# Cosine attention on one core: three score chunks exponentiated on VectorE, six K products on VectorE, four buffers of exponentials

## The chip, the core and the metric

The kernel runs on one core of a Trainium2 chip. The metric is the device time of one execution in microseconds, as the median of three runs. The engines are TensorE (PE; its weight loads are PEld), VectorE (DVE), ScalarE (ACT), GpSimd (POOL) and SyncE (SP), whose queue issues nearly all the transfers. Each engine works off its own queue strictly in order, and semaphores order the engines among each other.

## The reference

Q, K and V have shape (8, 12, 512, 64) in float32, and tau is 0.1.

```python
Q_norm = Q / (np.linalg.norm(Q, axis=-1, keepdims=True) + 1e-10)
K_norm = K / (np.linalg.norm(K, axis=-1, keepdims=True) + 1e-10)
scores = np.einsum('bhqd,bhkd->bhqk', Q_norm, K_norm) / tau
weights = np.exp(scores - np.max(scores, axis=-1, keepdims=True))
weights = weights / (np.sum(weights, axis=-1, keepdims=True) + 1e-10)
return np.einsum('bhqk,bhkd->bhqd', weights, V).astype(np.float32)
```

A score is a cosine divided by 0.1, so it lies within 10 of zero, and the kernel leaves out the maximum: a factor common to a row drops out when the row is divided by its sum.

## The kernel before

The 96 heads are worked in 48 pairs (0 to 47), two heads side by side on the 128 partitions. For one pair:

- LD and LV load Q, K and V (SP's queue). SQ squares Q and K (GpSimd, 1024 columns), SSQ sums the squares with eight matmuls against the identity into PSUM bank "x", and RED (VectorE) adds the rest, into a slot of the norm scratch bank nps.
- NEW is a chain of Newton steps on VectorE that turns sums into reciprocal norms, for a group of two pairs at once; it keeps its data in nps too. Pairs 0 to 2 go through LN and EX on ScalarE instead.
- SCL multiplies Q (w = 0, VectorE) and K (w = 1, GpSimd for most pairs) by their reciprocal norms. TR transposes both on TensorE into PSUM (banks "x" and "o1"), EVA copies them out to qt (VectorE, L504).
- SCO.s.c is score chunk c of 4: two matmuls of 512 columns, one for each head, on different halves of the array's rows, into two of the four banks of scps. EXP.s.c (ScalarE, L542) exponentiates the chunk, 1024 columns, into et. A SCO can start when the EXP two chunks before it is over.
- PV multiplies et by V, 32 matmuls of 65 columns (the 65th column is of ones and gives the row sums), into banks "o0" and "o1". VC (GpSimd) converts V to bf16 into vb beforehand. RCP and NRM (VectorE) divide and write ob; ST stores it.

A pair has four EXP, so ScalarE's order is a plain row of chunks. Buffers go round in rings: 18 of Q and K and of vb, 5 of qn and qt, 3 of et (R_ET).

The order of every queue is written out by hand in the table ORDER, one list of names for each engine. `schedule` (line 45) reads it; `run` (line 59) then makes the waits: an operation names what it needs, and gets a semaphore wait for each need on another engine (on TensorE and ScalarE, needs on the same engine are dropped; on VectorE they are kept). An operation with `take` waits for the last reader of the PSUM bank.

`split` (line 593) is in the kernel before and unused there, since SPLIT (line 675) is empty. It computes an exponential without ScalarE: a score product is added to a constant level, so that the float32 word holds, in its upper and lower halves, the integer and fractional part of the exponent, and four VectorE instructions evaluate a cubic on the lower half and write the result as the bits of a bf16 number.

Of the kernel before, what the change touches and what calls it, by code (L numbers as in the profile page):

```python
# [28 lines left out]
class Program:  # L29
# [95 lines left out]
def bass_cosine_similarity_attention_kernel(  # L125
# [16 lines left out]
    R_QK, R_V, R_SQ, R_QN, R_QT, R_ET, R_O = 18, 6, 6, 5, 5, 3, 8  # L142
# [8 lines left out]
    vb = sb("vb", [128, R_QK, NT, 2, DIM + 1], bf16)  # L151
# [11 lines left out]
    level = sb("level", [128, 128 + SEQ], bf16)  # L163
    wd = [sb(f"wd{i}", [128, SEQ], f32) for i in range(2)]
# [51 lines left out]
    def scored(s):  # L216

        if s < 0:
            return []
        last = [("SCO", s, NT - 1) if s else ("SCO", 0, 1, NT - 1)]  # L220
        return last + [("SCD", s, h) for h in range(2) if s in SPLIT]

# [204 lines left out]
    def pair(s):  # L427
# [24 lines left out]
        if 0 < s < LOGS:  # L452
# [9 lines left out]
            for w, dst in ((0, rq), (1, r)):  # L462
                exps(s, (w,), dst, xl[s][:, w], ("LN", s), gain, free)
            scaled(s, 0, "dve", rq, [("EX", s, 0), ("EX", s, 1)])
            for j in range(2) if s == 1 else ():
                scaled(1, 1, eng, r, [("EX", 1, w) for w in range(2)], (j,), slice(2 * j, 2 * j + 2))
            if s > 1:
                scaled(s, 1, eng, r, [("EX", s, w) for w in range(2)])
        elif s:
# [5 lines left out]
            else:  # L475
                free = [("EX", LOGS - 1, w) for w in range(2)]
# [39 lines left out]
        for c in range(NT) if s else ():  # L516
# [23 lines left out]
            else:  # L540
# [5 lines left out]
        P.add(("VC", s), "pool", [("LV", s), key("PV", s - R_QK, 1, NT - 1), "vone"],  # L546
              lambda e: e.tensor_scalar(  # L547
                  out=vb[:, iq, :, :, 0:DIM].rearrange("p c h d -> p h c d"),
# [5 lines left out]
        for c in range(NT) if s in CHUNKED else ():  # L554
            def pv(e, c=c):
                for h in range(2):
                    for t in range(NT):
                        last = e.matmul(  # L558
                            out=o_ps[:, h, 65 * t : 65 * t + 65],
                            lhsT=et[iet][:, c, h, 128 * t : 128 * t + 128], rhs=vb[:, iq, c, h, :],  # L560
# [3 lines left out]
            P.add(("PV", s, c), "pe", [("EXP", s, c), ("VC", s), ("PV", s, c - 1) if c else None], pv,  # L564
                  take=[] if c else ["o0", "o1"], until=("NRM", s))
        for h in range(2) if s not in CHUNKED else ():
            for t in range(NT):
                def pv(e, h=h, t=t):
                    for c in range(NT):
                        last = e.matmul(  # L570
                            out=o_ps[:, h, 65 * t : 65 * t + 65],
                            lhsT=et[iet][:, c, h, 128 * t : 128 * t + 128], rhs=vb[:, iq, c, h, :],
# [5 lines left out]
                      [("EXP", s, NT - 1) if s else ("EXP", 0, 1, 1), ("VC", s), before,  # L578
                       *([("EXD", s, h, 3)] if s in SPLIT else []),
# [13 lines left out]
    def split(s, c, ready, iqt, iet):  # L593

        for h in range(2):
            hs = slice(64 * h, 64 * h + 64)

            def scd(e, hs=hs):
                e.matmul(out=x_ps[:, :], lhsT=level[hs, 0:128], rhs=level[hs, 128 : 128 + SEQ], start=True, stop=False)
                return e.matmul(out=x_ps[:, :], lhsT=qt[iqt][hs, 1, c, :], rhs=qt[iqt][hs, 0, :, :], start=False, stop=True)  # L600

            P.add(("SCD", s, h), "pe", ready + ["level"], scd, take=["x"], until=("EXD", s, h, 3))
            w, done = wd[len(exd) % 2], exd[-2:-1]
            steps = [
                lambda e, w=w: e.tensor_scalar(
                    out=w[:, :], in0=y_u, scalar1=1.0, scalar2=-65536.0, op0=ALU.mult, op1=ALU.add),
                lambda e, w=w: e.tensor_tensor(out=w[:, :], in0=y_u, in1=w[:, :], op=ALU.mult),
                lambda e, w=w: e.scalar_tensor_tensor(
                    out=w[:, :], in0=y_u, scalar=65536.0 * CUBIC[1], in1=w[:, :], op0=ALU.add, op1=ALU.mult),
                lambda e, w=w, h=h: e.scalar_tensor_tensor(  # L610
                    out=et[iet][:, c, h, :].bitcast(u16), in0=w[:, :], scalar=128 * CUBIC[0] / 65536.0**3, in1=x_ps[:, :],
                    op0=ALU.mult, op1=ALU.add)]
            for k, step in enumerate(steps):
                P.add(("EXD", s, h, k), "dve",
                      [("EXD", s, h, k - 1) if k else ("SCD", s, h)] + (done if k == 0 else [])
                      + ([key("PV", s - R_ET, 1, NT - 1)] if k == 3 else []), step)
            exd.append(("EXD", s, h, 3))

    def final(s, iq, iet, io):
# [3 lines left out]
        for i, (h, lo, hi) in enumerate(ENDS):  # L623
            for c in range(NT):
                def pv(e, i=i, h=h, c=c, lo=lo, hi=hi):
                    for t in range(lo, hi):
                        last = e.matmul(
                            out=bank[i][:, 65 * t : 65 * t + 65],
                            lhsT=et[iet][:, c, h, 128 * t : 128 * t + 128], rhs=vb[:, iq, c, h, :],
# [5 lines left out]
                       scores_read(place[s, NT - 1] - 1) if i == 2 else None, ("VC", s),  # L635
# [23 lines left out]
    if FILL[1]:  # L659
# [14 lines left out]
ON = {'SQ.0.0.1': 'pool', 'SCL.2.1': 'dve', 'SCL.3.1': 'dve', 'LD.1.1': 'sp', 'SCL.1.1': 'dve'}  # L674
SPLIT = {}
# [8 lines left out]
        LD.0.0.0 LD.0.0.1 LD.1.0 LD.1.1 LD.2.0 LD.2.1 LD.3.0 LD.3.1 LD.4.1 LV.0 LD.4.0 LD.5.0 LD.5.1 LV.1 LD.6.1  # L684
        LD.6.0 LD.7.0 LD.7.1 LD.9.0 LV.2 LD.9.1 LD.8.0 LV.3 LD.10.0 LD.8.1 LV.6 LD.10.1 LV.4 LD.11.0 LV.5 LD.12.0
        LD.11.1 LV.8 LD.12.1 LD.14.0 LD.13.0 LD.13.1 LD.18.0 LD.14.1 LV.10 LV.7 LD.21.0 LD.16.0 LD.16.1 LD.15.0 LV.9
# [171 lines left out]
```

## Time and profile before

| | |
|---|---|
| median of 3 runs | 191.3 us (191.04 to 191.97) |
| span of the profiled execution | 189.4 us; its own time is not listed beside the span |
| granted TensorE clock | 0.996 |
| busy: PE, DVE, ACT, POOL | 174.1, 148.1, 181.7, 160.7 us |
| EXP (L542) | 184 of 1024 columns, 169.1 us busy |
| first EXP of pair 0, last of all | begins at 7.64 us, ends at 186.26 us |

Busy time is the union of an engine's instruction spans; an instruction's span reaches into that of the next, so a group's mean is longer than the distance from one start to the next. A busy PE is not a PE at its peak, because ends of matmuls are modelled. In a row of groups stand line, engine, operation, tiles and shapes, count, then busy time and mean ns of one, then the idle time before and what ended it. In a row of the timeline stand start, length and instruction.

### The profile page before, as it was taken

How to read it: one execution, taken by the hardware profiler on the slowest of the kernel's cores; microseconds unless marked ns; L12 is line 12 of the kernel's file. 1: busy time of each engine (PE TensorE's matmuls, PEld its weight loads, DVE VectorE, ACT ScalarE, POOL GpSimd, SP SyncE). 2: the span in 40 equal slices, each digit the busy share in tenths (PEclk: the TensorE clock that was granted, in tenths of full speed). 3: DMA queues.
4: the chain of work that ended last, by engine and by line, in shares of the span. 5: the costliest groups of instructions: out<-in, count | busy, mean ns of one | idle time of the engine just before them, and what ended most of it. 6: DMA issues, size and time to landing. Idle time of an engine off the chain costs nothing.

```text
span 189.4 us, 7341 instructions
## 1 busy us (share of the span) xinstructions
PE 174.1 (92%) x3078; PEld 110.7 (58%) x3078; DVE 148.1 (78%) x453; ACT 181.7 (96%) x210; POOL 160.7 (85%) x147
## 2 busy tenths in 40 slices
PE   7989998999999998999999999989989999987893
PEld 5446664665665665666555666556656666654552
DVE  1999987879877886898876968969888787787624
ACT  5699999999999999999999999999999999999993
POOL 1799999999999999999999999999997599562500
PEclk9999999999999999999999999999999999999998
DMA  6999999999469999999999959899959500754435
GB/s 169 338 352 349 350 350 349 350 376 383 151 197 356 291 345 315 269 376 323 359 361 378 271 167 336 257 332 345 328 160 313 168 12 9 211 177 140 141 107 173
DMA packets 52448, 50.80 MB, mean 268 GB/s; under 512 B 3136, under 2 KB 52416, under 8 KB 52416
## 3 DMA queue, kind: packets, MB, share of 16 engines
q1 hardware_dynamic: 51984, 50.02, 82.3%
q8 instruction: 24, 0.39, 0.9%
q10 hardware_dynamic: 432, 0.33, 0.6%
q14 instruction: 8, 0.07, 0.1%
HBM read 37.75 MB, written 12.58 MB: 266 GB/s over the span
## 4 chain that ended last, share of the span: by engine, by line
ACT 82%; DVE 7%; PE 7%; DMA 1%; issue 1%
ACT et L542 80%; PE scps L526 2%; DMA qk<-in_Q_dram 1%; DVE qn L296 1%; PE bps L570 1%; DVE ob L586 1%; DVE qt L504 1%; ACT et L371 1%; PE bps L339 1%; PE bps L558 1%; DVE nps L276 1%; PE bps L268 1%; DVE ob L643 1%; PE bps L498 0%; DVE xs L324 0%
## 5 line engine op out<-in xcount | busy, mean ns | idle before, releaser
L542 ACT ACTIVATE et<-scps 128x1024 bf16<-128x1024 f32 x184 | 169.1, 1128 | 0.5 <-PE scps L526 0.4
L250 POOL TENSOR_TENSOR sq<-qk 128x1024 bf16<-128x1024 f32 (+2 forms) x48 | 87.9, 1848 | 5.1 <-DMA qk<-in_Q_dram 4.9
L526 PE MATMUL scps<-qt 64*128 64x512 bf16 x376 | 74.4, 385 | 8.4 <-ACT et L542 6.1
L570 PEld LDWEIGHTS bps<-vb,et 128*128 128x128 bf16 x1472 | 51.4, 98 | 24.1 <-issue 18.0
L570 PE MATMUL bps<-vb,et 128*128 128x65 bf16 x1472 | 65.1, 194 | 0.2
L296 POOL TENSOR_TENSOR qn<-qk,rk 128x512 bf16<-128x512 f32 x44 | 45.8, 1051 | 11.8 <-DVE rk L405 11.7
L504 DVE COPY qt<-bps 128x1024 bf16<-128x1024 bf16 x46 | 31.8, 691 | 10.1 <-PE bps L498 9.4
L296 DVE TENSOR_TENSOR qn<-qk,nps 128x512 bf16<-128x512 f32 (+1 forms) x51 | 33.9, 671 | 0.8 <-ACT nps L286 0.2
L586 DVE TENSOR_TENSOR ob<-bps,rd 128x512 f32<-128x512 f32 x47 | 32.5, 691 | 1.2
L526 PEld LDWEIGHTS scps<-qt 64*128 64x128 bf16 x376 | 18.2, 93 | 25.3 <-ACT et L542 13.4
L547 POOL TENSOR_SCALAR vb<-vf 128x512 bf16<-128x512 f32 x48 | 29.9, 634 | 0.0
L268 PE MATMUL bps<-sq,ident 128*128 128x128 bf16 x376 | 29.1, 220 | 0.0
L268 PEld LDWEIGHTS bps<-sq,ident 128*128 128x128 bf16 x376 | 21.2, 98 | 9.4 <-issue 6.3
L584 DVE RECIPROCAL rd<-bps 128x8 f32<-128x8 f32 x47 | 9.7, 207 | 17.7 <-PE bps L570 14.3
L498 PE MATMUL bps<-ident,qn 64*128 64x64 bf16 x736 | 18.8, 191 | 2.4 <-DVE ob L586 0.4
L498 PEld LDWEIGHTS bps<-ident,qn 64*128 64x128 bf16 x736 | 14.2, 95 | 9.8 <-DVE nps L276 4.0
L276 DVE TENSOR_REDUCE nps<-bps 128x16 f32<-128x128 f32 x45 | 13.4, 297 | 1.8 <-PE bps L268 1.8
L397 DVE TENSOR_TENSOR nps<-nps,ys 128x32 f32<-128x32 f32 (+1 forms) x48 | 9.2, 193 | 0.9
L401 DVE SCALAR_TENSOR_TENSOR nps<-nps,ys 128x32 f32<-128x32 f32 (+1 forms) x48 | 9.1, 191 | 0.8
L237 PE MATMUL scps<-warm_in 128*128 128x256 bf16 x22 | 4.8, 402 | 1.1 <-DVE warm_in L232 1.1
L409 DVE TENSOR_SCALAR ys<-nps 128x32 int32<-128x32 int32 (+1 forms) x24 | 4.4, 183 | 0.5
L405 DVE SCALAR_TENSOR_TENSOR nps<-nps,ys 128x16 f32<-128x16 f32 (+1 forms) x25 | 4.3, 175 | 0.3
(44 smaller groups left out, 47.4 us busy)
## 6 DMA issues: line engine op xcount, KB each, us to landing
vf<-in_V_dram SPq DMA_DIRECT2D x48, 256.0 KB, 5.4
qk<-in_Q_dram SPq DMA_DIRECT2D x47, 256.0 KB, 5.9
qk<-in_K_dram SPq DMA_DIRECT2D x47, 256.0 KB, 5.7
out_dram<-ob SPq DMA_DIRECT2D x47, 256.0 KB, 4.4
qk<-in_Q_dram SPq DMA_DIRECT2D x2, 128.0 KB, 2.7
qk<-in_K_dram ACTq DMA_DIRECT2D x2, 128.0 KB, 2.9
out_dram<-ob SPq DMA_DIRECT2D x1, 128.0 KB, 2.2
out_dram<-ob SPq DMA_DIRECT2D x1, 64.0 KB, 1.9
```

Of the source, the lines that this page charges most:

```text
L250: emit = lambda e: e.tensor_tensor(out=b, in0=a, in1=a, op=ALU.mult)
L268: last = e.matmul(out=ps[:, 0:128], lhsT=ident[:, :], rhs=sq[s % R_SQ][:, :, 8 * k : 8 * k + 8], start=(k == 0), stop=(k == 7))
L276: lambda e: e.tensor_reduce(out=dst(None), in_=ps[:, 0:128].rearrange("p (w g e) -> p w g e", w=2, e=8), axis=AX.X, op=ALU.add))
L296: lambda e: e.tensor_tensor(out=o, in0=x, in1=r, op=ALU.mult))
L498: last = e.transpose(t_ps[:, k, b, :], qn[s % R_QN][ks, b // NT, b % NT].rearrange("p h d -> p (h d)"), ident[ks, ks])
L504: lambda e, lo=lo, hi=hi: e.tensor_copy(out=qt[iqt][:, :].rearrange("p w t (k x) -> p k (w t) x", k=2)[:, :, lo:hi], in_=t_ps[:, :, lo:hi]))
L526: last = e.matmul(out=sc_ps[:, 2 * b + k, :], lhsT=qt[iqt][64 * h : 64 * h + 64, 1, n, :], rhs=qt[iqt][64 * h : 64 * h + 64, 0, :, :], sta ...
L542: lambda e, c=c, b=b: e.activation(out=et[iet][:, c, :, :], in_=sc_ps[:, 2 * b : 2 * b + 2, :], func=ACT.Exp, scale=scale, bias=bias))
L547: lambda e: e.tensor_scalar(out=vb[:, iq, :, :, 0:DIM].rearrange("p c h d -> p h c d"), in0=vf[iv][:, :, :].rearrange("p h (c d) -> p h c ...
L570: last = e.matmul(out=o_ps[:, h, 65 * t : 65 * t + 65], lhsT=et[iet][:, c, h, 128 * t : 128 * t + 128], rhs=vb[:, iq, c, h, :], start=(c = ...
L584: lambda e: e.reciprocal(out=rd[io][:, :], in_=grid[:, :, :, DIM]))
L586: lambda e: e.tensor_tensor(out=ob[io][:, :], in0=grid[:, :, :, 0:DIM], in1=rd[io][:, :].unsqueeze(3).to_broadcast([128, 2, NT, DIM]), op= ...
```

## The change

1. SPLIT names chunk 1 of pairs 13, 25 and 37. ScalarE's list loses EXP.13.1, EXP.25.1 and EXP.37.1, and TensorE's the three SCO. The other three chunks of these pairs get a bias (SHIFT) that puts them on the scale of the cubic.
2. `split` works in pieces of one head h and half of the queries j: four pieces of 256 columns for a pair. For each, TensorE does SCD (two products of 256 columns on the same 64 rows, the level and the score, summed in the upper half of the scratch bank nps), and VectorE does the four steps EXD.s.h.j.0 to 3.
3. `schedule` makes SCD wait for the VectorE operation on the scratch bank (RED, NEW, SCL or EXD) that stands last before step 0 in VectorE's list, and step 0 waits for SCD.
4. The K products of pairs 8, 10, 17, 20, 29 and 32 go from GpSimd to VectorE. Where the other pair of the group stays on GpSimd, the last Newton step is issued in two pieces (six more).
5. et has four buffers instead of three, vb nine instead of 18; level and wd are smaller.
6. Pairs 1 and 2: the reciprocal norms of Q and K come from one EX each instead of two.
7. All five lists of ORDER are new, the head's among them.

```diff
     def schedule(self):
...
+        last = None
+        for o in order["dve"]:
+            if o.key[0] == "EXD" and o.key[-1] == 0:
+                self.ops[("SCD", *o.key[1:-1])].needs.append(last)
+            if o.key[0] in ("RED", "NEW", "SCL", "EXD"):
+                last = o.key
...
-    R_QK, R_V, R_SQ, R_QN, R_QT, R_ET, R_O = 18, 6, 6, 5, 5, 3, 8
+    R_QK, R_V, R_SQ, R_QN, R_QT, R_ET, R_O, R_VB = 18, 6, 6, 5, 5, 4, 8, 9
...
-    y_u = x_ps[:, :].bitcast(u16).rearrange("p (x two) -> p x two", two=2)[:, :, 0]
+    y_ps = n_ps[:, 256:512]
+    y_u = y_ps.bitcast(u16).rearrange("p (x two) -> p x two", two=2)[:, :, 0]
...
-            for w, dst in ((0, rq), (1, r)):
-                exps(s, (w,), dst, xl[s][:, w], ("LN", s), gain, free)
+            both = eng == "dve"
+            for w, dst in ((0, spare[:, 16 * s - 8 : 16 * s + 8]),) if both else ((0, rq), (1, r)):
+                exps(s, (w,), dst, xl[s][:, :, :].rearrange("p w x -> p (w x)") if both else xl[s][:, w], ("LN", s), gain, free)
...
-        P.add(("VC", s), "pool", [("LV", s), key("PV", s - R_QK, 1, NT - 1), "vone"],
+        P.add(("VC", s), "pool", [("LV", s), key("PV", s - R_VB, 1, NT - 1), "vone"],
...
+            for j in range(2):
+                hs, qs = slice(64 * h, 64 * h + 64), slice(256 * j, 256 * j + 256)
+                def scd(e, hs=hs, j=j):
+                    e.matmul(out=y_ps, lhsT=level[hs, 0:128], rhs=level[hs, 128:384], start=True, stop=False)
+                    return e.matmul(
+                        out=y_ps, lhsT=qt[iqt][hs, 1, c, :], rhs=qt[iqt][hs, 0, 2 * j : 2 * j + 2, :], start=False, stop=True)
+                P.add(("SCD", s, h, j), "pe", ready + ["level"] + exd[-1:], scd)
+                w = wd[len(exd) % 2][:, :]
+                steps = [
+                    lambda e, w=w: e.tensor_scalar(
+                        out=w, in0=y_u, scalar1=1.0, scalar2=-65536.0, op0=ALU.mult, op1=ALU.add),
+                    lambda e, w=w: e.tensor_tensor(out=w, in0=y_u, in1=w, op=ALU.mult),
+                    lambda e, w=w: e.scalar_tensor_tensor(
+                        out=w, in0=y_u, scalar=65536.0 * CUBIC[1], in1=w, op0=ALU.add, op1=ALU.mult),
+                    lambda e, w=w, h=h, qs=qs: e.scalar_tensor_tensor(
+                        out=et[iet][:, c, h, qs].bitcast(u16), in0=w, scalar=128 * CUBIC[0] / 65536.0**3, in1=y_ps,
+                        op0=ALU.mult, op1=ALU.add)]
...
-SPLIT = {}
+SPLIT = {13: 1, 25: 1, 37: 1}
```

The K products are the names SCL.8.1, SCL.10.1, SCL.17.1, SCL.20.1, SCL.29.1 and SCL.32.1, added to the table ON. Of the new lists, these are the stretches of the head and of pair 13:

```text
sp, head:    LD.0.0.0 LD.1.1 LD.0.0.1 LD.1.0 LD.2.1 LD.2.0 ...
             (before: LD.0.0.0 LD.0.0.1 LD.1.0 LD.1.1 LD.2.0 LD.2.1 ...)
act, head:   SQ.0.1.0 SQ.0.0.0 SQ.0.1.1 SQ.1.1.1 LN.0.0 EX.0.0 SQ.1.0 LN.0.1 EX.0.1 EXP.0.0.0 LN.1 EXP.0.0.1 EX.1.0 ...
             (before: SQ.0.0.0 SQ.0.1.0 SQ.0.1.1 LN.0.0 EX.0.0 LN.0.1 EX.0.1 SQ.1.0 SQ.1.1.1 EXP.0.0.0 EXP.0.0.1 LN.1 EX.1.1 EX.1.0 ...)
dve, head:   RED.0.1.0 RED.0.0.0 RED.0.1.1 SQ.1.1.0 SCL.0.0.0 SCL.0.1.0 RED.0.0.1 EVA.0.0.0 EVA.0.1.0 SCL.0.0.1 SCL.0.1.1 RED.1.0 ...
             (before: RED.0.0.0 RED.0.1.0 RED.0.1.1 SCL.0.0.0 SCL.0.1.0 RED.0.0.1 EVA.0.0.0 EVA.0.1.0 SCL.0.0.1 SQ.1.1.0 SCL.0.1.1 ...)
pe, head:    TR.0.0.0 TR.0.1.0 fill.0 fill.1 fill.2 SSQ.1 SCO.0.0.0 SCO.0.0.1 TR.0.0.1 TR.0.1.1 ...
             (before: TR.0.0.0 TR.0.1.0 fill.0 fill.1 fill.2 SCO.0.0.0 SCO.0.0.1 TR.0.0.1 SSQ.1 TR.0.1.1 ...)
dve, pair 13: EVA.13 EXD.13.0.0.0 EXD.13.0.0.1 RED.17 EXD.13.0.0.2 NEW.8.0 EXD.13.0.0.3 RCP.10 NRM.10 EXD.13.0.1.0 NEW.8.1
             EXD.13.0.1.1 EVA.14 EXD.13.0.1.2 NEW.8.2 EXD.13.0.1.3 EVA.15 EXD.13.1.0.0 NEW.8.3 EXD.13.1.0.1 NEW.8.4
             EXD.13.1.0.2 NEW.8.5 RED.18 NEW.8.7 NEW.8.6 RCP.11 EXD.13.1.0.3 NEW.8.8 NRM.11 EXD.13.1.1.0 RED.19
             EXD.13.1.1.1 SCL.16.0 EXD.13.1.1.2 RCP.12 NEW.9.0 NRM.12 NEW.9.1 EXD.13.1.1.3 NEW.9.2 EVA.16
pe, pair 13: SCO.11.3 TR.13 SCO.12.0 PV.10.0 SCD.13.0.0 SCO.12.1 SSQ.17 SCO.12.2 PV.10.1 SCO.12.3 SCD.13.0.1 SCO.13.0 TR.14
             PV.11.0 (half) SCO.13.2 PV.11.0 (half) SCO.13.3 TR.15 SCD.13.1.0 SCO.14.0 SSQ.18 PV.11.1 (part) SCO.14.1
             PV.11.1 (rest) SCO.14.2 SSQ.19 SCD.13.1.1 SCO.14.3 PV.12.0 (part) SCO.15.0 PV.12 (rest) SCO.15.1 SCO.15.2 TR.16
             SCO.15.3 PV.13.0 SCO.16.0 PV.13.1 ...
pool:        ... SQ.20.0 VC.17 SQ.22.0 SQ.21.0 VC.22 VC.18 SCL.18.1 SCL.19.1 ...
```

More of the change, by code (lines that the diff above doesn't have):

```diff
@@ L220, in scored @@
         last = [("SCO", s, NT - 1) if s else ("SCO", 0, 1, NT - 1)]
-        return last + [("SCD", s, h) for h in range(2) if s in SPLIT]
+        return last + [("SCD", s, h, j) for h in range(2) for j in range(2) if s in SPLIT]
     P.add("one", "pool", [], lambda e: e.memset(ones[:, :], 1.0))
@@ L595, in split @@
         for h in range(2):
[L596 to L617, printed above, removed]
+            for j in range(2):
[15 more added lines that the diff above has]
+                        op0=ALU.mult, op1=ALU.add)]
+                for k, step in enumerate(steps):
+                    P.add(("EXD", s, h, j, k), "dve",
+                          [("EXD", s, h, j, k - 1) if k else ("SCD", s, h, j)]
+                          + ([key("PV", s - R_ET, 1, NT - 1)] if k == 3 else []), step)
+                exd.append(("EXD", s, h, j, 3))
```

320 lines of the change are left out of this document (168 added, 152 removed).

## The prediction

> **What bounds the kernel now.** I read the page first, then the chain of waits, then the windows.
>
> ```profile
> span 189.4 us, 7341 instructions
> PE 174.1 (92%) x3078; PEld 110.7 (58%) x3078; DVE 148.1 (78%) x453; ACT 181.7 (96%) x210; POOL 160.7 (85%) x147
> ACT 82%; DVE 7%; PE 7%; DMA 1%; issue 1%
> ```
>
> ScalarE (ACT) is the fullest engine and holds 82% of the chain that ended last. The pieces of that chain show how evenly:
>
> ```profile
> 29.06 130.32 ACT et L542 x142
> 159.41 22.11 ACT et L542 x24
> 181.57 0.60 PE scps L526 x2
> ```
>
> From 29.06 to 181.52 us the chain is exponentials of L542 and nothing else. One of them takes 130.32/142 = 0.918 us of the chain; the 1128 ns of the group's row below is one instruction with its overlap into the next, so it is not the price. A chunk taken off ScalarE is worth 0.918 us for as long as the other engines keep up. Whether they can is read from the windows (columns: PE, PEld, DVE, ACT, POOL, then clock and DMA):
>
> ```profile
> 10.00:180.00 170.00, 159.34 (x2929) 102.08 (x2928) 139.03 (x428) 169.46 (x188) 156.24 (x137) 1.00 0.86 276
> 20.00:140.00 120.00, 112.83 (x2088) 72.64 (x2085) 98.67 (x302) 119.52 (x132) 119.21 (x104) 1.00 0.97 312
> ```
>
> ScalarE is idle for 0.54 us in 170. VectorE (DVE) is idle for 31.0. GpSimd (POOL) has 0.8 in the 120 us up to 140. Work goes from the first to the second, and a little from the third to the second.
>
> **What a VectorE instruction costs.** Groups with shapes kept apart:
>
> ```profile
> L542 ACT ACTIVATE et<-scps 128x1024 bf16<-128x1024 f32 x184 | 169.1, 1128 | 0.5 <-PE scps L526 0.4
> L526 PE MATMUL scps<-qt 64*128 64x512 bf16 x376 | 74.4, 385 | 8.4 <-ACT et L542 6.1 <-DVE qt L311 0.4 <-issue 0.3
> L296 POOL TENSOR_TENSOR qn<-qk,rk 128x512 bf16<-128x512 f32 x44 | 45.8, 1051 | 11.8 <-DVE rk L405 11.7
> L296 DVE TENSOR_TENSOR qn<-qk,nps 128x512 bf16<-128x512 f32 x49 | 33.2, 681 | 0.6 <-ACT nps L286 0.2
> L586 DVE TENSOR_TENSOR ob<-bps,rd 128x512 f32<-128x512 f32 x47 | 32.5, 691 | 1.2
> L504 DVE COPY qt<-bps 128x1024 bf16<-128x1024 bf16 x46 | 31.8, 691 | 10.1 <-PE bps L498 9.4
> L276 DVE TENSOR_REDUCE nps<-bps 128x16 f32<-128x128 f32 x45 | 13.4, 297 | 1.8 <-PE bps L268 1.8
> L584 DVE RECIPROCAL rd<-bps 128x8 f32<-128x8 f32 x47 | 9.7, 207 | 17.7 <-PE bps L570 14.3 <-PE bps L558 2.6
> L397 DVE TENSOR_TENSOR nps<-nps,ys 128x32 f32<-128x32 f32 x42 | 8.2, 195 | 0.9
> L405 DVE SCALAR_TENSOR_TENSOR rk<-nps,ys 128x16 f32<-128x16 f32 x21 | 3.5, 168 | 0.2
> L296 DVE TENSOR_TENSOR qn<-qk,nps 128x256 bf16<-128x256 f32 x2 | 0.8, 417 | 0.1
> L643 DVE TENSOR_TENSOR ob<-nps,rd 128x256 f32<-128x256 f32 x1 | 0.4, 425 | 0.0
> ```
>
> Packed instructions overlap, as the VectorE timeline shows:
>
> ```profile
> 43.49 0.69 DVE L586 TENSOR_TENSOR ob<-bps,rd 128x512 f32<-128x512 f32 x1
> 44.12 0.30 DVE L276 TENSOR_REDUCE nps<-bps 128x16 f32<-128x128 f32 x1
> 44.33 0.68 DVE L296 TENSOR_TENSOR qn<-qk,nps 128x512 bf16<-128x512 f32 x1
> 44.93 0.69 DVE L504 COPY qt<-bps 128x1024 bf16<-128x1024 bf16 x1
> 45.54 0.18 DVE L409 TENSOR_SCALAR ys<-nps 128x32 int32<-128x32 int32 x1
> ...
> 53.44 0.19 DVE L397 TENSOR_TENSOR nps<-nps,ys 128x32 f32<-128x32 f32 x1
> 53.54 0.29 DVE L276 TENSOR_REDUCE nps<-bps 128x16 f32<-128x128 f32 x1
> ```
>
> From start to start a normalisation takes 0.63, a reduction 0.21, a scaling 0.60, a copy 0.61, a Newton step with independent work behind it 0.10: each is its duration less 0.06 to 0.09. An exponential step of 256 columns isn't in the trace. The nearest rows are the two 256-column ones at 417 and 425 ns, so I take 0.42 alone and 0.33 when other work follows. Its first three steps read every second 16-bit word of PSUM. No row has that, so I bound a step by half the columns (0.29, which is 0.42 less half of the 0.27 between 256 and 512) and by a 512-column row (0.69). I take the row of the right width; at 0.69 each split pair would get 12 x 0.27 = 3.2 us more.
>
> **The change part by part.**
>
> ScalarE loses three chunks: 3 x 0.918 = **-2.75 us**.
>
> VectorE gains 48 steps (15.8 at 0.33, 20.2 at 0.42), six K products (3.6 to 4.1) and six more Newton pieces (0.6 to 1.0): 20 to 25 us. In a window shortened to about 167 us it then has 159 to 164 us of work, and 3 to 8 us of idle time where it had 31. That is the heart of the matter. GpSimd loses 6 x 1.051 = 6.3 us, cover and no gain.
>
> The load is not spread evenly, so I count the order of pair 13. Between the copies EVA.13 and EVA.16 VectorE is given 16 steps (5.4), twelve Newton steps (1.3), three reductions (0.6), three reciprocals and normalisations (2.3), three copies (1.8) and a scaling (0.6): **12.0 to 12.3 us**. TensorE's order puts 14 score chunks between the transposes that these copies follow: 14 x 0.918 = 12.85 us. It fits, with half a microsecond over. From EVA.15 to EVA.20 the same count gives 20.1 against 21 chunks, 19.3 us: 0.8 too much, taken up if copies slip towards the scores that need them.
>
> What else waits: each scaling or reduction or Newton step that precedes a step 0 must be over before its score product SCD writes the scratch bank. SCD stands in TensorE's queue directly ahead of SCO.12.1, SCO.13.0, SCO.14.0 and SCO.14.3 (for pair 13), and ScalarE waits for those. So VectorE and TensorE meet twelve times. Each meeting costs VectorE the time h that the work put between (a normalisation or a copy, about 0.6 to 0.9) doesn't cover. The nearest rows are VectorE's other waits for TensorE: 10.1/46 = 0.22 per copy, 17.7/47 = 0.38 per reciprocal. I take h = 0.33: 12.3 + 4 x 0.33 = 13.6 against 12.85 + 0.5. That 0.5 is how late a score may come: 0.918 less the 0.385 of its matmul. About 0.27 is left per pair: **+0.8 us** for three pairs. Bounds: 0, and 3 x (12.3 + 4 x 0.92 - 13.35) = 7.9 when each meeting waits a whole chunk.
>
> TensorE: an SCD is two products of 256 columns on the same 64 rows, which cannot run side by side. Two of 512 on the same rows took 0.60 at 181.57 above, so 0.3 to 0.6, times 12, less three chunks of 0.385: 2.4 to 6.0 us over three stretches of some 13. I cost it at nothing beyond h, since scores there wait for ScalarE (6.1 us in the L526 row).
>
> The fourth buffer of exponentials lets the steps write while PV of the pair three back still reads; nine V buffers instead of 18 make each conversion wait for PV nine pairs back. GpSimd has VC.22 ahead of VC.18 and SCL.18.1; it waits for PV.13, which stands four chunks before TR.18. Nothing, while PV.13 isn't late by over a chunk. Loads and stores stand in a new order throughout; the bytes are the same, the DMA share of 0.97 up to 140 us stays, and the groups above show no wait for a load: nothing.
>
> **The head** is reordered. Its rows:
>
> ```profile
> 3.48 1.20 ACT L248 ACTIVATE sq<-qk 128x256 bf16<-128x256 f32 x3 [0.50 <-DMA qk<-in_Q_dram]
> 5.17 0.75 DVE L333 TENSOR_TENSOR qn<-qk,bps 128x256 bf16<-128x256 f32 x2
> 6.63 0.55 PE L237 MATMUL scps<-warm_in 128*128 128x256 bf16 x3
> 7.21 0.60 PE L366 MATMUL scps<-qt 64*128 64x512 bf16 x2
> 7.41 0.41 DVE L250 TENSOR_TENSOR sq<-qk 128x256 bf16<-128x256 f32 x1
> 7.64 1.08 ACT L371 ACTIVATE et<-scps 128x512 bf16<-128x512 f32 x2
> 8.09 0.62 PE L268 MATMUL bps<-sq,ident 128*128 128x128 bf16 x8
> 9.07 0.22 ACT L282 ACTIVATE xl<-xs 128x16 f32<-128x16 f32 x1 [0.35 <-DVE xs L276]
> 9.32 0.28 ACT L286 ACTIVATE nps<-xl 128x8 f32<-128x8 f32 x2
> 11.69 0.28 ACT L286 ACTIVATE nps<-xl 128x8 f32<-128x8 f32 x2
> ```
>
> SQ.1.1.1 moves ahead of the first logarithm (0.40 on ScalarE, and 0.41 of SQ.1.1.0 on VectorE beside it), so the scaling at 5.17 starts about 0.4 later. SSQ.1 moves ahead of the first score at 7.21: about 0.55 more. The first exponential goes from 7.64 to about 8.6. Given back: the 0.35 wait at 9.07, and one small exponential of 0.14 for each of two pairs. Net +0.3; LD.1.1, now second in SP's queue, may hold the logarithm a little longer. I take **+0.4** (-0.3 to +0.9). Nine chunk exponentials of the split pairs get a nonzero bias; the two small ones of pair 1 (bias zero, at 9.32) and of pair 2 (not zero, at 11.69) both take 0.28, so that costs nothing.
>
> **The sum**: 189.4 - 2.75 + 0.4 + 0.8 = 187.85 us of span. The page gives the profiled execution no time but its span; the median of the runs is 1.9 above it, and I carry that over: **189.7 us**.
>
> [...]
>
> **Rivals.**
>
> *Clean gain, 188.5.* The meetings are covered (h under 0.25) and the head comes out even: 189.4 - 2.75 + 1.9 = 188.55. For it: 12.3 fits into 12.85. Against: idle time of 31 us has to fall to under 8.
>
> *Nothing left, 191.3.* h = 0.46, half a chunk: 3 x (12.3 + 1.84 - 13.35) = 2.4, and the head's 0.4 takes the rest.
>
> ```profile
> DVE qt L504 <- PE bps L498: 9.4, 22, 0.8
> ```
>
> For it: where a copy did wait for its transposes, it was 0.43 on the mean (9.4 us in 22 waits). Against: over all copies it is the 0.22 above.
>
> *The meetings decide, 194.2.* At h = 0.7 each split pair holds ScalarE up by 1.75: 189.4 - 2.75 + 0.4 + 5.25 + 1.9. It is slower than before by half a per cent from h = 0.54. For it: TensorE is parked at an SCD with scores behind it, then VectorE waits for TensorE, each in order. Against: SCD stands next to a score every time and work stands between.
>
> *VectorE doesn't overlap, 194.8.* With whole durations the stretch is 6.7 + 12 x 0.19 + 3 x 0.30 + 3 x 0.90 + 3 x 0.69 + 0.68 = 15.3, late by 1.95 three times: 5.85. The step at 44.12, which starts 0.06 before its forerunner's end, speaks against it. [...]
>
> *TensorE sets the pace, 192.4.* If its 159.3 of 170 us were all needed, a stretch of 13 us has some 0.7 free; four SCDs of 0.55 less one chunk add 1.8 to it: 1.15 too much, three times, 3.5.
>
> ```profile
> 63.62 0.62 PE L268 MATMUL bps<-sq,ident 128*128 128x128 bf16 x8
> 64.18 0.39 PE L526 MATMUL scps<-qt 64*128 64x512 bf16 x2
> ```
>
> Against it: a score that follows eight sums starts 0.06 before their modelled end, so busy is not full.
>
> **How the numbers follow.** Forecast 0.46, clean 0.20, nothing left 0.14, meetings 0.12, TensorE 0.05, no overlap 0.03. Half a per cent (0.96 us) is about what can be told from no change here. Faster by more: all but a twelfth of the forecast, and the clean case: 0.62. Within: 0.19. Slower: the last three, nearly: 0.19. The forecast's own range is 189.0 to 190.4. The range that should hold 8 in 10 goes from 187.9 (clean, with the head's -0.3 and a little) to 192.4 (TensorE's case), which leaves out the meetings, the missing overlap, the steps at 0.69 and the lowest few per cent.
>
> **What would show it.** Right: three L542 instructions fewer with a pace still near 0.92; the first exponential near 8.6; steps near 0.42; VectorE over 90% busy; ScalarE's waits for L526 grown by about a microsecond around pairs 13, 25 and 37. Wrong: waits of several microseconds there, VectorE's waits for the SCD line of half a microsecond or more each, steps well off 0.42, or the first exponential before 7.7.

## The result, and the profile after

The changed kernel takes **193.9 us** (192.5 to 196.1) where the one before takes 191.3: a ratio of 1.012, 95% interval 1.008 to 1.016. The longest execution, 196.1 us at a granted clock of 0.974, belongs to a slower state and isn't counted in the ratio. By the ratio the kernel is slower by 2.3 us; 189.7 was forecast. The profiled execution took 193.8 us with a span of 191.7, so the 1.9 us around the span that the forecast carried over was about right (it was 2.1), and the loss lies inside.

The page of the changed kernel: span, busy times, chain that ended last.

```profile
span 191.7 us, 7421 instructions
...
PE 176.4 (92%) x3096; PEld 111.9 (58%) x3096; DVE 164.2 (86%) x515; ACT 180.8 (94%) x205; POOL 154.3 (80%) x141
...
PE 36%; ACT 30%; DVE 20%; POOL 10%; issue 2%; DMA 2%; ACTq 0%; POOLq 0%
```

ScalarE held 82% of the chain before and holds 30% now. The chain used to be an unbroken row of exponentials; now it has 399 pieces instead of 113 and changes engine all along the run. ScalarE's timeline shows what that does to its pace. First the kernel before, then the changed one (L542 is now L551):

```profile
12.81 15.88 ACT L542 ACTIVATE et<-scps 128x1024 bf16<-128x1024 f32 x17
29.06 153.37 ACT L542 ACTIVATE et<-scps 128x1024 bf16<-128x1024 f32 x167 [0.37 <-PE scps L526]
```

```profile
14.39 110.54 ACT L551 ACTIVATE et<-scps 128x1024 bf16<-128x1024 f32 x118
125.21 17.67 ACT L551 ACTIVATE et<-scps 128x1024 bf16<-128x1024 f32 x19 [0.28 <-PE scps L535]
143.28 8.40 ACT L551 ACTIVATE et<-scps 128x1024 bf16<-128x1024 f32 x9 [0.40 <-PE scps L535]
```

From start to start a chunk took (153.37 - 1.02) / 166 = 0.918 us; it takes (110.54 - 1.02) / 117 = 0.936, and the rows behind it begin with waits of 0.28 and 0.40. Over all full chunks up to pair 46 the distances sum to 168.5 us in 183 steps before (0.921) and 169.4 in 180 after (0.941). So two things were lost: the row of full chunks **begins 1.58 us later** (14.39 against 12.81), and it is **0.0205 us slower at each of 180 steps, 3.7 us**. Against them stand the three chunks, 2.75. That is +2.5, less 0.2 by which the end after pair 46 is shorter, and the span grew by 2.3.

The groups of the changed kernel:

```profile
L551 ACT ACTIVATE et<-scps 128x1024 bf16<-128x1024 f32 x181 | 168.6, 1048 | 1.9 <-PE scps L535 0.9
...
L535 PE MATMUL scps<-qt 64*128 64x512 bf16 x370 | 73.9, 385 | 5.3 <-ACT et L551 4.2
...
L617 DVE TENSOR_SCALAR wd<-nps 128x256 f32<-128x256 uint16 x12 | 5.0, 418 | 1.5 <-PE scps L535 1.0
```

The idle column of ScalarE shows almost nothing (1.9 us), although 3.7 us are lost. 144 of its 180 steps are under 0.93 us, and there an exponential starts 0.14 us before its forerunner's end on the mean; the one that starts 0.997 after its forerunner's start, 0.08 late, still starts 0.03 before that end, so it only loses overlap and is not counted as idle. The mean duration fell too, from 1128 ns to 1048, while the work of one is the same, but it doesn't measure the loss: chunks that start in time fell as much (by the starts and lengths in the traces from 1133 to 1053 ns), and 80 ns for each of 181 would be 14 us. Only the distances from start to start show what was lost. The split itself behaves as counted: a step 0 (L617) takes 418 ns, and the twelve of them wait 1.5 us together.

### The profile page after: what moved, and what is told of

Read it like the earlier page. It is cut to its first block, busy times and chain, and to the rows that moved or that the text cites. A ratio compares the mean times of both kernels' runs of the same rounds, so it can differ in the third digit from the quotient of the medians.

```text
span 191.7 us, 7421 instructions
## 1 busy us (share of the span) xinstructions
PE 176.4 (92%) x3096; PEld 111.9 (58%) x3096; DVE 164.2 (86%) x515; ACT 180.8 (94%) x205; POOL 154.3 (80%) x141
## 4 chain that ended last, share of the span: by engine, by line
PE 36%; ACT 30%; DVE 20%; POOL 10%; issue 2%; DMA 2%; ACTq 0%; POOLq 0%
ACT et L551 28%; PE bps L580 13%; PE scps L535 11%; POOL sq L257 6%; PE bps L275 5%; DVE ob L596 5%; PE bps L507 4%; DVE qn L303 3%; DVE qt L513 2%; POOL qn L303 2%; POOL vb L556 2%; DMA qk<-in_K_dram 2%; DVE nps L283 2%; DVE rd L594 1%; ACT et L378 1%
## 5 line engine op out<-in xcount | busy, mean ns | idle before, releaser
L551 ACT ACTIVATE et<-scps 128x1024 bf16<-128x1024 f32 x181 | 168.6, 1048 | 1.9 <-PE scps L535 0.9
L580 PEld LDWEIGHTS bps<-vb,et 128*128 128x128 bf16 x1472 | 51.7, 98 | 22.2 <-issue 13.9
L303 POOL TENSOR_TENSOR qn<-qk,rk 128x512 bf16<-128x512 f32 x38 | 39.3, 1045 | 11.4 <-DVE nps L412 5.4
L303 DVE TENSOR_TENSOR qn<-qk,nps 128x512 bf16<-128x512 f32 (+1 forms) x57 | 37.5, 669 | 0.2 <-ACT nps L293 0.2
L556 POOL TENSOR_SCALAR vb<-vf 128x512 bf16<-128x512 f32 x48 | 29.4, 628 | 0.3 <-PE bps L580 0.3
L275 PEld LDWEIGHTS bps<-sq,ident 128*128 128x128 bf16 x376 | 21.8, 99 | 9.8 <-issue 5.1
L378 ACT ACTIVATE et<-scps 128x1024 bf16<-128x1024 f32 (+1 forms) x5 | 4.1, 847 | 2.6 <-PE scps L373 2.6
L617 DVE TENSOR_SCALAR wd<-nps 128x256 f32<-128x256 uint16 x12 | 5.0, 418 | 1.5 <-PE scps L535 1.0
```

Of the source, the lines that this page charges most:

```text
L275: last = e.matmul(out=ps[:, 0:128], lhsT=ident[:, :], rhs=sq[s % R_SQ][:, :, 8 * k : 8 * k + 8], start=(k == 0), stop=(k == 7))
L303: lambda e: e.tensor_tensor(out=o, in0=x, in1=r, op=ALU.mult))
L551: lambda e, c=c, b=b: e.activation(out=et[iet][:, c, :, :], in_=sc_ps[:, 2 * b : 2 * b + 2, :], func=ACT.Exp, scale=scale, bias=bias))
L556: lambda e: e.tensor_scalar(out=vb[:, s % R_VB, :, :, 0:DIM].rearrange("p c h d -> p h c d"), in0=vf[iv][:, :, :].rearrange("p h (c d) -> ...
L580: last = e.matmul(out=o_ps[:, h, 65 * t : 65 * t + 65], lhsT=et[iet][:, c, h, 128 * t : 128 * t + 128], rhs=vb[:, s % R_VB, c, h, :], star ...
```

## The experiments

Names used below: a *stretch* is TensorE's work from one full score chunk to the next in its list, that chunk included. By the rows of the traces a PV group counts 0.12 us, SSQ 0.55, TR 0.26 to 0.35, a score chunk 0.32, SCD 0.35. *Late* is how far a chunk starts behind its forerunner's start plus 0.918. Each ratio is to the kernel before, run on the same chip.

| version | median us | ratio, 95% interval |
|---|---|---|
| changed kernel | 193.9 | 1.012 (1.008 to 1.016) |
| old head | 191.9 | 1.004 (1.001 to 1.007) |
| four more warm-up matmuls | 192.3 | 1.005 (1.002 to 1.009) |
| no split | 194.6 | 1.015 (1.007 to 1.024) |
| no split and old head ("lists") | 194.3 | 1.018 (1.015 to 1.021) |
| lists of before, new buffers | 191.2 | 1.000 (0.998 to 1.002) |
| before with six long stretches | 193.0 | 1.011 (1.006 to 1.015) |
| stretches cut to 1.1 / to 1.16 | 197.5 / 195.3 | 1.031 (1.023 to 1.039) / 1.024 (1.018 to 1.031) |
| before with SCO.40.3 earlier | 190.9 | 0.999 (0.997 to 1.001) |

**The head: two versions.** "Old head" is the changed kernel with the first 7 to 44 entries of each list in the order of before; the other adds only matmuls on warm-up data ahead of the first real one.

```diff
 "sp":  LD.0.0.0
-  LD.1.1 LD.0.0.1 LD.1.0
+  LD.0.0.1 LD.1.0 LD.1.1
 "act": table
-  SQ.0.1.0 SQ.0.0.0 SQ.0.1.1 SQ.1.1.1 LN.0.0 EX.0.0 SQ.1.0 LN.0.1 EX.0.1 EXP.0.0.0
+  SQ.0.0.0 SQ.0.1.0 SQ.0.1.1 LN.0.0 EX.0.0 LN.0.1 EX.0.1 SQ.1.0 SQ.1.1.1 EXP.0.0.0
 "pe":  fill.0 fill.1 fill.2
-  SSQ.1 SCO.0.0.0 SCO.0.0.1 TR.0.0.1
+  SCO.0.0.0 SCO.0.0.1 TR.0.0.1 SSQ.1
```

> The changed kernel with the head's order of before in all five lists (up to the last exponential of pair 0), everything else as changed. In the two traces the first chunk of pair 1 is exponentiated at 12.81 us before and at 14.39 us after, 1.58 us later. If ScalarE is full from there on, undoing the head gives these 1.6 us back: about 192.3 us. If what follows is held by VectorE or TensorE and not by ScalarE, the gain is taken by longer waits behind it: about 193.9 us.

```diff
-WARM = 19
+WARM = 23
```

> The changed kernel with 23 warm-up matmuls instead of 19. TensorE sat idle for 0.99 us before the first transposes (0.30 before the change), and its matmuls from there to 10 us take nearly twice as long as before the change (eight sums 1.06 us against 0.62, two scores 1.03 against 0.60). If the idle time causes that, four more warm-up matmuls (0.9 us) close it, the first exponential moves from 9.57 to about 8.7, and the time falls to about 193.0 us. If the slow matmuls come from something else (the new order, the loads beside them), nothing changes: 193.9 us.

Both gave back most of the head's 1.58 us: the row of full chunks began at 12.22 with the old head and at 12.80 with four more warm-up matmuls (14.39 before them), and the time fell by 0.8 and 0.7 per cent, 1.5 and 1.3 us. TensorE's timeline shows where the time went. First the changed kernel, then the same with four more warm-up matmuls:

```profile
4.28 1.06 PE L244 MATMUL scps<-warm_in 128*128 128x256 bf16 x4
6.33 1.06 PE L346 MATMUL bps<-ident,qn 128*64 128x128 bf16 x8 [0.99 <-DVE qn L340]
7.33 0.82 PE L244 MATMUL scps<-warm_in 128*128 128x256 bf16 x3
7.94 1.06 PE L275 MATMUL bps<-sq,ident 128*128 128x128 bf16 x8
8.94 1.03 PE L373 MATMUL scps<-qt 64*128 64x512 bf16 x2
```

```profile
4.77 0.71 PE L244 MATMUL scps<-warm_in 128*128 128x256 bf16 x5
6.41 0.74 PE L346 MATMUL bps<-ident,qn 128*64 128x128 bf16 x8 [0.93 <-DVE qn L340]
7.08 0.50 PE L244 MATMUL scps<-warm_in 128*128 128x256 bf16 x3
7.42 0.61 PE L275 MATMUL bps<-sq,ident 128*128 128x128 bf16 x8
7.96 0.60 PE L373 MATMUL scps<-qt 64*128 64x512 bf16 x2
```

The order of the work is the same in both, and both have an idle time of about 0.95 us before the first transposes (the logarithm came 0.66 later: a square more stands ahead of it, and the squares wait 0.68 for a load of K; that the K load of pair 1, now second in SP's queue, is the reason is not shown). But everything behind it takes 1.4 to 1.75 times as long in the first: 1.06 against 0.61 for the same eight sums, 1.03 against 0.60 for a score. In the kernel before, the idle time there was 0.30 us, and the sums took 0.62 and the score 0.60.

What raised the pace in the second trace is another matter. Its warm-up matmuls follow each other every 0.213 us up to the 17th and every 0.11 us from there on, at 4.6 us; the first of the four added ones, the 20th, starts only at 4.88. So in this execution the full pace came before the added work could bring it. The moment differs between executions: with the head of before and 19 warm-up matmuls it lies between 4.0 and 6.8 us in thirteen traces, with the new head and 19 at 10.1, 10.2 and 10.3 us in three (stretches cut to 1.1, no split, changed kernel). That four more matmuls help rests on the times alone, 1.005 against 1.012 with intervals that just overlap; that they help by closing the idle time is not shown.

**Without the split.** The three chunks go back to ScalarE as ordinary chunks; the second version has the old head too.

```diff
-SPLIT = {13: 1, 25: 1, 37: 1}
+SPLIT = {}
 "dve": (EXD.13, EXD.25, EXD.37 taken out)
 "pe":  (SCD taken out, SCO.13.1, SCO.25.1, SCO.37.1 put back)
```

> The changed kernel with the three chunks back on ScalarE: SPLIT empty, no score product or exponential step for VectorE, the chunk's two matmuls and its exponential put back in the lists, everything else (order, K products, buffers, head) as changed. ScalarE has 2.75 us more to do. If the scattered late chunks come from the lists, they stay, but for the 0.4 us or so around pairs 13 to 16, 25 to 28 and 37 to 40: about 196.2 us. If they come from VectorE's load or the meetings, ScalarE's lost time falls from 4.5 us to the 0.6 of the kernel before: about 192.8 us.

> The changed kernel with the head in the order of before and with the three split chunks back on ScalarE as ordinary chunks; the six K products stay on VectorE. So ScalarE has the work of before, VectorE 4 to 5 us more, GpSimd 6.3 us less, and the lists after the head have the new order. If the new order makes the scattered late chunks: 192.5 to 193.2 us, ratio to the kernel before 1.007 to 1.012, ScalarE's lost time about 4 us with late chunks at 8.2, 16.1, 18.3, 30.3, 33.3, 38.1, 41.0 and 43.1. If the exponentials on VectorE made them: 190.8 to 191.5, as before.

ScalarE's timeline of the version without split, whose second row has as many chunks as that of the kernel before:

```profile
30.91 156.03 ACT L551 ACTIVATE et<-scps 128x1024 bf16<-128x1024 f32 x167 [0.43 <-PE scps L535]
```

The same 167 exponentials take 156.03 us instead of 153.37: **0.934 a chunk without any split**. So most of the lateness comes with the new lists, not with the exponentials on VectorE, which added 0.8 us to it with the new head and 1.6 with the old one, by the sums of distances. The late chunks sit at the same places with and without split: 8.2, 16.1, 18.3, 30.3, 33.3, 38.1, 41.0, 43.1. The split alone is worth 2.0 us of span with the new head (193.7 to 191.7) and 1.5 with the old one (191.3 to 189.8). By the medians it is 0.6 and 2.4 us; the four times without split are 193.6, 193.7, 195.4 and 195.5, and the profile is of the last. Both medians, 194.6 and 194.3, fit neither of the times expected for their two cases (the second is nearer to the case of the lists); what decides is the pace and the places in the traces. The profile of "lists" is the fastest of its six runs, so the spans rather understate what the lists cost: 1.9 us by them, 3.4 by the medians.

**The same places on TensorE.** The chain of waits at chunk 43.1 of the changed kernel (start, us, what); in "lists" the same pieces follow one another:

```profile
169.00 0.36 PE scps L535 x2
169.36 1.08 PE bps L580 x32
170.44 0.34 PE scps L535 x2
170.78 0.02 issue
170.80 1.94 ACT et L551 x2
```

All 32 products of PV.41 stand between SCO.43.0 and SCO.43.1: a stretch of 1.4 us, without one wait in it. ScalarE starts 43.1 0.25 late. The kernel before had two stretches above 1.3 us (3.1 and 40.3), and those were two of its three latest chunks (0.28 and 0.40 us; its chain breaks at 159.38 for the second):

```profile
154.80 4.58 ACT et L542 x5
159.38 0.02 issue
159.41 2.85 ACT et L542 x3
```

The changed list has nine stretches above 1.3 us and some seventeen above 1.2, where it was two and three (the second pair of counts shifts by a few with what a PV group next to a score is counted at).

Not every late chunk is one of these. In the changed kernel's profile the latest, 35.3 by 0.57 us, is a wait of TensorE for squares from GpSimd:

```profile
142.29 0.62 PE L275 MATMUL bps<-sq,ident 128*128 128x128 bf16 x8 [0.57 <-POOL sq L257]
```

Chunks that are late by more than 0.05 add up to 2.4 us in the kernel before and 5.3 in the changed one. At stretches above 1.2 us stand 0.7 and 2.5 to 3.0 of it, at shorter ones in which TensorE waited for another engine 0.7 and 1.9. So about two thirds of what was added go with the long stretches.

**Are stretches the cause? Put into the kernel before.** Six score chunks stand later in its TensorE list, for example:

```diff
 "pe":  SCO.18.2 PV.16.0.3 PV.16.1.0 PV.16.1.1 PV.16.1.2 PV.16.1.3
-  SCO.18.3 SSQ.23 SCO.19.0
+  SSQ.23 SCO.18.3 SCO.19.0
```

> The kernel before, with nothing changed but six places of TensorE's list: SCO.8.2, 14.2, 18.3, 22.2, 33.3 and 38.1 each stand behind some more products PV than they did, so that TensorE's work from one score chunk to the next is a single stretch of 1.36, 1.40, 1.49, 1.40, 1.36 and 1.36 us (by the durations of the traces: PV group 0.12, SSQ 0.55, TR 0.26 to 0.35, score chunk 0.32) and the next stretch is 0.32. The total work is the same. Theory (a stretch of TensorE's list above about 1.16 us makes ScalarE wait for what is above, and it doesn't get it back): the six chunks start 0.2 to 0.33 us late each, 1.4 us in all, and the kernel takes 192.2 to 192.9 us where the one before takes 191.1. Rival (the average load of TensorE is what counts, lumps are taken up by the two score banks): no change, 191.0 to 191.4, and none of the six chunks is late by over 0.1. Second rival: the late chunks of the changed kernel come from VectorE, and lumps alone give less than 0.5 us.

The ratio is 1.011, about 2.0 us, a little above the expected 1.1 to 1.8. All six chunks are late now: 8.2, 14.2, 18.3, 22.2, 33.3 and 38.1 by 0.38, 0.42, 0.43, 0.75, 0.17 and 0.33, where the kernel before had none of them over 0.1. The chain at 18.3 of this version:

```profile
80.05 0.32 PE scps L526 x2
80.37 0.72 PE bps L570 x20
81.08 0.46 PE bps L268 x8
81.55 0.34 PE scps L526 x2
81.89 0.02 issue
81.91 1.94 ACT et L542 x2
```

(22.2 is later than its stretch alone: the second half of PV.20, moved ahead, waited there for VectorE.) The profiled execution took 195.5 us, more than the median, because 5.1 to 6.3 were late too, by 2.9 together: there TensorE was idle for 1.55 us and slow behind it, as the last section shows, at a place where nothing was moved. The six chunks lie outside that time. The same work in longer pieces makes ScalarE late: the theory holds for the kernel before.

**Can they be taken out of the changed kernel?** Two versions, one that cuts nearly every stretch to about 1.1 us, and one, with the old head, that cuts fifteen of the seventeen to 1.12 to 1.16 and moves PV alone, such as:

```diff
 "pe":  SCO.43.0 PV.41.0.0 PV.41.0.1 PV.41.0.2 PV.41.0.3 PV.41.1.0 PV.41.1.1
-  PV.41.1.2 PV.41.1.3 SCO.43.1
+  SCO.43.1 PV.41.1.2 PV.41.1.3
```

> The changed kernel with score chunks put earlier in TensorE's list, past PV, sums and transposes, so that no stretch between two chunks of one list holds more than about 1.1 us of TensorE's work; nothing else moves. Counted from rows (a PV group of four matmuls 0.12, eight sums 0.55, a transpose 0.3, a score chunk 0.32), stretches over 1.2 us were 3 before, are 17 after the change, and 4 in this kernel. If these long stretches make the scattered late chunks, ScalarE's lost time between pairs 1 and 46 falls from 4.5 us to about 2, and the time to about 191.5 us. If the exponentials on VectorE, its fullness or the meetings at the scratch bank make them, the time stays at 193.9 us.

> The changed kernel with the head in the order of before (that one took 191.9 us), and fifteen of the seventeen stretches of TensorE's list that are longer than 1.2 us cut to 1.12 to 1.16 by moving one or two products PV to the neighbouring stretch, which stays under 1.15. Transposes, sums of squares and products SCD keep their places. Theory (long stretches make the late chunks): most of the late chunks there are gone, lost time of ScalarE falls from 5.6 to 3 to 4 us, and the kernel takes 189.6 to 190.8, less than the one before. Rival (each PV that is moved makes VectorE or GpSimd late somewhere else, as in the version with all stretches under 1.1, 197.5 us): 191.9 or more, with new waits of TensorE for VectorE.

Both made it worse. The waits of TensorE (us in total, times, longest), of the first version, the second, the changed kernel, and the kernel before:

```profile
PE bps L507 <- DVE ob L596: 3.1, 6, 0.8
PE scps L535 <- ACT et L551: 2.6, 9, 0.5
PE bps L580 <- DVE ob L596: 1.3, 6, 0.3
```

```profile
PE scps L535 <- ACT et L551: 4.1, 11, 0.8
PE bps L507 <- DVE ob L596: 1.8, 4, 0.8
```

```profile
PE bps L507 <- DVE ob L596: 1.2, 4, 0.6
```

```profile
PE scps L526 <- ACT et L542: 6.1, 18, 0.5
...
PE bps L498 <- DVE ob L586: 0.4, 1, 0.4
```

A PV that stands one score later makes the division behind it (RCP, NRM, `ob`) later; the copies that stand behind that in VectorE's list come late too, and transposes then wait for their bank (1.2 us in the changed kernel, 3.1 and 1.8 here). My reading, which no run separates, is that the long stretches are where this list keeps VectorE fed. The same in small, in the kernel before:

```diff
 "pe":  PV.38.1.0 PV.38.1.1 PV.38.1.2 PV.38.1.3
-  SSQ.45 SCO.40.3
+  SCO.40.3 SSQ.45
```

> The kernel before with one exchange in TensorE's list: SCO.40.3 one place ahead of SSQ.45, so that the stretch in front of it falls from 1.36 to 0.79 us and the next is 0.87 in place of 0.32. In the trace of before EXP.40.3 starts 0.40 us late there. Theory of the long stretch: the 0.40 is gone, and the kernel is 0.3 to 0.4 us faster than the one before (ratio 0.998). Rival (the later sum of squares, 0.32 us, is handed on through VectorE and comes back as a late transpose): no change, and a new late chunk in pairs 44 to 46.

No change (0.999), as its rival said, only sooner: 40.3 is in time, and the 0.40 comes back at once in pair 41 (41.1 late by 0.26, 41.2 by 0.12), where TR.42 waits 0.33 for the reduction behind the later SSQ.45.

**Buffers and halves of the order.** The first of these has the code of the changed kernel without split and all lists of before; in the next, TensorE's and VectorE's lists after the head are those of the changed kernel; in the last, all lists are. In all three the operations stand on their engines of before, so that the six K products are GpSimd's again.

```diff
-ON = {..., 'SCL.8.1': 'dve', 'SCL.10.1': 'dve', 'SCL.17.1': 'dve', 'SCL.20.1': 'dve', 'SCL.29.1': 'dve', 'SCL.32.1': 'dve'}
-SPLIT = {13: 1, 25: 1, 37: 1}
+ON = {...}
+SPLIT = {}
```

> The code of the changed kernel with four buffers of exponentials and nine of V, no split, and all five lists as in the kernel before. If the buffers cost nothing, as forecast: ratio 0.998 to 1.002, 190.7 to 191.4 us. If nine V buffers make conversions wait for PV and so GpSimd late: above 191.8.

> The version with all lists of before and the buffers of the changed kernel, but with TensorE's and VectorE's lists after the head in the order of the changed kernel. If the long stretches of TensorE's new order make the late chunks: 192.6 to 194.4 us, at the places named above. If the order of loads and of GpSimd carries the loss: 190.9 to 191.6.

> The operations of the kernel before, each on its engine of before, with the head of before: no split, the six K products on GpSimd, at the places among its neighbours that they have in the list of before. Only the order of the lists after the head and the numbers of buffers (four of exponentials, nine of V) are those of the changed kernel. If the order carries the loss: 193.0 to 194.6 us, ratio 1.011 to 1.019, with the late chunks of the version with K on VectorE (8.2, 16.1, 18.3, 30.3, 33.3, 38.1, 41.0, 43.1). If the K products on VectorE carry it: 190.9 to 191.6. If GpSimd's list again has no room for them: above 195 with waits of over 1 us for qn or sq from GpSimd.

*Buffers*: 1.000 (0.998 to 1.002). Nothing, as forecast. *TensorE's and VectorE's order alone*: 1.031, 197.2 us. More than expected, because GpSimd's old list serves the new one badly (waits of 0.9 and 1.0 us for squares at 7.2 and 9.2, and 0.9 for a K product at 33.1). But the late chunks are there again, each by the same amount: its chain at 43.1 reads

```profile
173.55 1.08 PE bps L580 x32
174.63 0.34 PE scps L535 x2
174.97 0.02 issue
175.00 1.02 ACT et L551
```

and 16.1, 18.3, 41.0 and 43.1 are late by 0.24, 0.20, 0.18 and 0.25, as with the split, without it, and with either order of GpSimd: these places go with TensorE's and VectorE's lists, and not with the K products, which are GpSimd's in this version and in the next. *All of the order, K products on GpSimd*: 1.052, 201.1 us, the third case of its expectation: GpSimd holds 29% of the chain, and TensorE waits 3.0 us at TR.34. So the K products on VectorE are not what the new lists pay for; without them these lists run worse. Two versions in which the K products went back at later places of GpSimd's list, with and without the split, took 199.5 and 199.9 us (1.045 and 1.047), with transposes that wait over 2 us for them. The other half of the order (GpSimd's and SP's new lists with TensorE's and VectorE's of before) took 212.3 us (1.104). Each half costs more with the other's partner than both together: the price cannot be put down to one list, only the late places can.

**A version that might have beaten both** took pair 13's split with the middle of the new lists, and the rest from the kernel before. It took 194.1 us (1.015, 1.013 to 1.018); its profile, of an execution of 198.8 us, has a transpose that waits 2.0 us for VectorE where the lists are joined, around pair 9. None of the versions is faster than the kernel before by more than can be told.

## Why the prediction was wrong

- **Three chunks, -2.75: right.** 181 exponentials, each still worth 0.918 where nothing holds it up. The split bought 1.5 to 2.0 us of span net (0.6 to 2.4 by the medians); the forecast's -2.75 + 0.8 is 1.95.
- **Steps and meetings: right in kind.** A step took 0.42, and 0.29 to 0.34 from start to start where other work followed (0.33 forecast); a meeting cost VectorE 0.125 on the mean (1.5 us in twelve), where I took h = 0.33. VectorE was busy for 92 of the 100 us between 50 and 150. "ScalarE's waits grown by a microsecond around pairs 13, 25 and 37" did not come as forecast: of the 0.8 to 1.6 us that the split adds, only 0.12 at 13.2 and 0.24 at 23.0 stand in both profiles with it. The changed kernel has 0.39 at 31.0 and 0.57 at 35.3 besides, which the version with the old head, split too, doesn't have. *The meetings decide* fell: no wait for an SCD result of over half a microsecond.
- **"I cost it at nothing beyond h, since scores there wait for ScalarE": this step failed.** I took the 6.1 us for which TensorE's scores wait (now 4.2) as room, and looked for trouble only where something was added. The sum had no term for the order of the lists elsewhere; for loads and stores I wrote that a new order costs nothing, and TensorE's new order I did not count at all. It could have been counted before: stretches above 1.3 us went from two to nine. By the counts above TensorE's work grew from about 0.77 to 0.80 us a chunk, and without the split it is 0.77 as before, which on average leaves room; what ran out was the room in single stretches. Measured: +3.7 us over the run in the profile, 2.4 to 2.9 of it without any split.
- **My tolerance ("0.5 is how late a score may come")** was set against one late score. ScalarE had next to nothing to make up a late chunk with: in neither profile do two full chunks start less than 0.903 us apart, against the 0.918 of the undisturbed row. The changed kernel's profile has 15 that are late by over 0.15, where there were four.
- **The head, +0.4: right in kind, mis-sized.** Measured: first exponential at 9.57 (8.6 forecast), row of full chunks +1.58. I added up what stands ahead of the first score at the durations of before. What was missing is that those durations would not hold: TensorE's matmuls took up to 1.75 times as long until 10.3 us. In the trace in which they kept their durations, with four more warm-up matmuls, the first exponential began at 8.39, close to the forecast, and the row of full chunks at 12.80.
- **Buffers, at nothing: right** (1.000).
- Of the rivals, *TensorE sets the pace* (192.4, chance 0.05) came nearest in kind: TensorE leads the chain (36%). But it set three overfull stretches of 13 us at the split pairs, and the loss lies over the whole run. My argument against it, that a busy TensorE isn't a full one, holds for the mean (0.77 to 0.80 us of counted work in a chunk's 0.918) and says nothing on a stretch. That the time of *The meetings decide* (194.2) is close to the measured one is chance, since the meetings waited little.

What stays open: whether the new lists would gain by fewer long stretches, since every version in which I moved them by hand lost more elsewhere, so that the cause is shown in the kernel before and by the places of the late chunks, not by a cure; and what brings the full pace of the head sooner.

## What to carry to other kernels

Where one engine sets the pace and has no slack (before, ScalarE was idle for 0.54 us in 170), count the work of its feeder **between each two of its deliveries**, not the mean load: here six longer stretches with the same total work cost about 2.0 us, and the changed kernel's profile counts 1.9 us idle where 3.7 were lost; the distances from start to start show them. A hand-written set of in-order lists is one fitted piece: here moves that looked free in TensorE's list came back through VectorE (197.5 us from 193.9, 195.3 from 191.9), so after any reordering compare the pace of the bounding engine over the whole run, not at the place of the edit. In the head here the durations of matmuls did not carry over from one order of the work to the other: eight sums took 1.06 us where they had taken 0.62.

## What the runs showed of the hardware

TensorE's matmuls of one shape did not always take the same time, and in the head the granted clock of a window doesn't show it. In the changed kernel's head eight sums took 1.06 us in place of 0.61, while the windows there have a granted clock of 1.00 (columns: PE, PEld, DVE, ACT, POOL, clock, DMA share, GB/s):

```profile
8.00:10.00 2.00, 2.00 (x12) 0.97 (x11) 0.80 (x3) 0.42 (x1) 1.49 (x3) 1.00 1.07 365
```

The clock's record in this trace begins at 10.33 us, with full speed, and what lies before the first entry is shown as 1.00. In four traces, that with 23 warm-up matmuls among them (4.60 us), the first entry falls among the warm-up matmuls, and at that moment they go from 0.213 us apart to 0.11.

In the version with all of the new order and the K products on GpSimd, matmuls in mid-run took longer too, behind an idle time of 3.0 us at 134.8, and there the clock column, 0.54, shows it:

```profile
134.42 0.39 PE L535 MATMUL scps<-qt 64*128 64x512 bf16 x2
137.81 0.41 PE L507 MATMUL bps<-ident,qn 64*128 64x64 bf16 x16 [3.00 <-POOL qn L303]
138.04 0.49 PE L535 MATMUL scps<-qt 64*128 64x512 bf16 x2
138.46 1.06 PE L580 MATMUL bps<-vb,et 128*128 128x65 bf16 x16
139.46 0.61 PE L535 MATMUL scps<-qt 64*128 64x512 bf16 x2
```

```profile
138.00:141.00 3.00, 3.00 (x49) 2.14 (x42) 1.37 (x5) 1.92 (x2) 3.00 (x4) 0.54 0.97 310
```

A score took 0.61 instead of 0.39, sixteen products 1.06 instead of 0.67, for some 3.5 us. By these two pairs that is the work of about 2.2 us (3.5 x 0.39/0.61), so I estimate that 1.3 us were lost behind the wait of 3. Behind an idle time of 1.0 us in mid-run (in the version with TensorE's and VectorE's order alone, at 45) the sums took 0.62, as elsewhere. Between these the length of the idle time alone doesn't tell which it will be. In the version with the K products back and no split (199.9 us), in one execution, 16 transposes kept their 0.41 us behind 2.07 us of idle time and took 0.61 behind 1.75:

```profile
72.55 0.41 PE L507 MATMUL bps<-ident,qn 64*128 64x64 bf16 x16 [2.07 <-POOL qn L303]
119.13 0.61 PE L507 MATMUL bps<-ident,qn 64*128 64x64 bf16 x16 [1.75 <-POOL qn L303]
```

The kernel before with six long stretches was slow behind an idle time of 1.55 us, up to 29.80: eight sums took 0.95 us, and the clock was 0.56 in the two microseconds from 30 on.

These two slow stretches of mid-run last 3.41 and 3.42 us in the clock's record (138.22 to 141.63 with all of the new order, 30.24 to 33.66 with six long stretches). The warm-up matmuls begin at 1.10 us in the kernel before, in the changed one, with the old head and with 23 of them; the full pace came 2.9 to 5.7 us later with the head of before, 3.5 later with 23 of them, and 9.2 later in the changed kernel, with 19 and an idle time of 0.99 us behind them.
